# Plain transposes of rows scaled on VectorE, and shifted ticks, in a hybrid encoder trunk

## The chip, the cores and the metric

The kernel runs on one core of a Trainium2 chip. The metric is the device time of one execution in microseconds (us). A core has five engines, each with its own instruction queue that is worked off in order: TensorE (PE in the profile, with PEld for its weight loads), VectorE (DVE), ScalarE (ACT), GpSimd (POOL) and SyncE (SP), which only issues DMAs. Engines wait for one another by semaphores.

## The reference

One layer of a trunk over a sequence of 2048 rows of 1024 numbers, in float32:

```
xn = rmsnorm(x, g1)
u, q, f, i, o, gates = split(xn @ w_in)          # 512 each, gates 2 x 1024
ya = pool_mixer(u) @ w_pa                        # trailing means over 2, 4, 8, 16 rows, minus the row
yb = hgrn2(silu(q), f, i, silu(o)) @ w_pb        # gated linear recurrence, 4 heads of 128
merged = sigmoid(gate_a) * ya + sigmoid(gate_b) * yb
x  = x + merged @ w_o
h  = causal depthwise conv (width 3) of rmsnorm(x, g2) @ w_up    # 2 x 2816 columns
x  = x + (silu(gate half of h) * value half of h) @ w_down
out = rmsnorm(x, final_g)
```

`rmsnorm(x, g) = x * rsqrt(mean(x*x) + eps) * g`, row by row. The recurrence is `S_t = diag(f_t) S_{t-1} + (1 - f_t) i_t^T`, with the output `S_t^T q_t`, normalised and multiplied by silu(o).

## The kernel before

**Tiling.** The sequence is cut into two super-blocks of 1024 rows, and each of these into two halves of 512 rows (four tiles of 128 rows, `NT`). For each super-block `mixer` runs (the input projection, pooling, the recurrence, the two branches, the output projection `wo`), and then `ffn` (the up projection, convolution and gate, the down projection `dn`, and the last norm). The big products go by a scheme of seven products in place of eight on 2x2 blocks, P1 to P7 (`ORDER`, `IO_ORDER`); its operands are forms of the normalised, transposed rows of the two halves: B11 and B21 of the first half, B22 and the sums T1 to T4 of both.

**Precision.** Each operand is split into a high and a low part (the names end in `h` and `l`), and each product is three matmuls, high by high, high by low, low by high, of 128x512. Weights are loaded by SP into `raw`, and converted into `ops` by one instruction on ScalarE (L206, high) and one on VectorE (L207, low). A product of a unit (`Unit.multiply`) is twelve such matmuls: four steps of k by three.

**Order.** Products are written out in order, and their matmuls go through `mm` (L145), which counts them; after every sixth one it calls `tick`. A tick first converts the next weight, at most `LOOKAHEAD` = 4 products ahead, and then steps the tasks: generators, whose `yield n` leaves n ticks before they go on. The tasks issue the forms, the pooling, the recurrence and the last norm between the products' matmuls. The compiler's scheduler then puts each engine's instructions into a final order.

**Norm and transposes.** `norm_rows` takes four tiles of 128 rows (two tiles of 128x512 each): ScalarE squares and sums them (L636, into a tile `junk` that nobody reads), POOL adds the two sums (L637) and makes the reciprocal root (L629, L630), and POOL makes a diagonal matrix of it (L649, `x_dg` or `m_dg`, 128x128). `transpose` then is an ordinary matmul of a 128x128 piece of the rows with the diagonal (L656): it scales and transposes at once, into a PSUM bank (`x_t`, `m_t`). There are eight such blocks of 512 rows: x0 to x3, ahead of the input projection, and m0 to m3, ahead of the up projection, each with 4 x 8 transposes. `forms_a_task` makes the first half's forms, splits included, and `forms_b_task` the second half's (T1 and T2 by L714 from PSUM, then the splits, L607 and L608).  For x0 the transposes are issued row tile by row tile into eight banks (`early`); for the second halves they wait for a signal, `go`, which `ffn` gives ahead of its product number `GO_AT` (`go_up`) and `proj_io` in its second product (`go_io`).

**The gate and value projection.** `proj_io` computes the recurrence's values v and output gates z row-wise, four banks (one for each j) to a product; after P7 it takes `u3 = Z - e1` (L1150, `io_u`), which frees the bank Z for P4's matmuls, and adds it to bank V for z (`out_z`, L999).

**The recurrence.** `hgrn_task` runs eight times in each super-block (four heads, two halves), three at a time. It starts from q and the forget factors f, prepares copies and products on ScalarE and VectorE (L828 to L832), yields, and issues its first products on TensorE (L905, `pl`); its later plain transposes are `pk` (L940) and `pt` (L983), done as `pe.transpose` against the identity.

The functions that the change touches, as they stand:

Of the kernel before, what the change touches and what calls it, by code (L numbers as in the profile page):

```python
# [11 lines left out]
F32 = mybir.dt.float32  # L12
F32R = mybir.dt.float32r
U8 = mybir.dt.uint8
AF = mybir.ActivationFunctionType
ALU = mybir.AluOpType
AX = mybir.AxisListType

P = 128
# [11 lines left out]
NT = TB // P  # L31
# [25 lines left out]

M_ORDER = (0, 4, 1, 5, 2, 6, 3, 7)

N_SLOTS = 80  # L60
N_RUN = 3
N_HEADS = 2
GO_AT = 2
LEAD = 5
X_AT, X_AT2 = 1, 4
GO_IO = (("P2", 1), ("P2", 0))
# [8 lines left out]
MM_PER_TICK = 6  # L75
# [3 lines left out]
def tile_trunk(  # L79
# [16 lines left out]
    pe, act, dve, pool, sp = nc.tensor, nc.scalar, nc.vector, nc.gpsimd, nc.sync  # L96

    const = ctx.enter_context(tc.tile_pool(name="const", bufs=1))
    small = ctx.enter_context(tc.tile_pool(name="small", bufs=8))
    rawp = ctx.enter_context(tc.tile_pool(name="rawp", bufs=N_RAW))  # L100
    opsp = ctx.enter_context(tc.tile_pool(name="opsp", bufs=N_OPS))
    slots = ctx.enter_context(tc.tile_pool(name="slots", bufs=N_SLOTS))
    diags = ctx.enter_context(tc.tile_pool(name="diags", bufs=8))
    dram = ctx.enter_context(tc.tile_pool(name="dram", bufs=1, space=bass.MemoryType.DRAM))
    banks = ctx.enter_context(tc.tile_pool(name="banks", bufs=8, space=bass.MemoryType.PSUM))

    def slot(name, cols=TB, dt=F32):
        return slots.tile([P, cols], dt, tag="s", name=name, padded_shape=[P, 528])

    def bank(name, cols=512):  # L110
        return banks.tile([P, cols], F32, tag="b", name=name, padded_shape=[P, 512])
# [6 lines left out]
    count = [0, None]  # L118
# [15 lines left out]
    def tick():  # L134
        stream.advance(1)
        for t in list(tasks):
            t.wait -= 1
            if t.wait <= 0 and t.live:
                t.step()
# [5 lines left out]
    def mm(*args, **kw):  # L145
        count[1] = pe.matmul(*args, **kw)  # L146
        count[0] += 1
        if count[0] % MM_PER_TICK == 0:
            tick()


# [364 lines left out]
    ident = const.tile([P, P], F32, tag="ident", name="ident")  # L516
# [30 lines left out]
    inv = const.tile([P, 4, 16], F32, tag="inv", name="inv")  # L547
    uhist = const.tile([P, 4, 16], F32, tag="uhist", name="uhist")
    hist = const.tile([P, 2 * MF, 2], F32, tag="hist", name="hist")
    junk = const.tile([P, 512], F32, tag="junk", name="junk")  # L550
    fmask = const.tile([P, 2, 64], F32, tag="fmask", name="fmask")
    state = {}
    state_at = {(0, h) for h in range(HEADS)}
    for h in range(HEADS):
# [65 lines left out]
    def n_step(ps, w, xk, j, first, last, **kw):  # L620
        xh, xl = xk
        a, b = xh[:, j * P : (j + 1) * P], xl[:, j * P : (j + 1) * P]
        mm(ps, a, w[:, 0], start=first, stop=False, **kw)
        mm(ps, a, w[:, 1], start=False, stop=False, **kw)
        mm(ps, b, w[:, 0], start=False, stop=last, **kw)

    def rstd_of(ssq, n, scale, name):
        r = small.tile([P, 4], F32, tag="rstd", name=name)
        pool.tensor_scalar(r[:, :n], ssq, scale, EPS, ALU.mult, ALU.add)  # L629
        pool.tensor_tensor(r[:, :n], r[:, :n], neghalf[:, :n], ALU.pow)  # L630
        return r

    def row_rstd(halves, name):
        ss = small.tile([P, 4], F32, tag="ssq", name=name + "ss")
        for hf in range(2):
            act.activation(junk, halves[hf], AF.Square, accum_out=ss[:, hf : hf + 1])  # L636
        pool.tensor_tensor(ss[:, 2:3], ss[:, 0:1], ss[:, 1:2], ALU.add)  # L637
        return rstd_of(ss[:, 2:3], 1, 1.0 / D, name + "r")

    def norm_rows(src, name, xs, after, lag=1):  # L640
        for j in range(NT):
            while (src, j) not in ready:
                yield 1
            halves = [xt[src, j, c] for c in range(2)]
            r = row_rstd(halves, f"{name}{j}")
            if lag:
                yield lag
            dg = diags.tile([P, P], F32, tag="dg", name=f"{name}dg{j}")
            pool.tensor_scalar(dg, ident, r[:, 0:1], None, ALU.mult)  # L649
            xs[j] = halves, dg  # L650
            after(j)

    def transpose(ps, xs, j, k):
        c = (k % 4) * P
        halves, dg = xs[j]
        pe.matmul(ps[:, j * P : (j + 1) * P], halves[k // 4][:, c : c + P], dg,  # L656
                  start=True, stop=True)

    def transposed(xs, k, name, gain, ps=None):
        if ps is None:  # L660
# [101 lines left out]
    def need(forms, key, late):  # L762
        while len(forms[key]) < 4:
            late.step()
        return forms[key]
# [45 lines left out]
    def hgrn_task(b, h, d, q, vd, zd, od):  # L811
# [18 lines left out]
        dve.tensor_tensor(q1[:, :, 0], qo, do, ALU.mult)  # L830
        dve.tensor_tensor(qe, qe, de, ALU.mult)
        dve.tensor_tensor(qo, q1[:, :, 0], de, ALU.mult)  # L832
        yield 3
        def mask(key, n):
            m = masks[key]
            return m.unsqueeze(1).to_broadcast([P, n, m.shape[1], m.shape[2]])
# [114 lines left out]
        ss = slot(f"ss{b}_{h}")  # L951
# [11 lines left out]
        for c in range(NT):  # L963
            o_ = po[:, c * P : (c + 1) * P]
            pe.matmul(o_, att[:, c * P : (c + 1) * P], vt[:, c * P : (c + 1) * P],
                      start=True, stop=False)
# [3 lines left out]
        for c in range(NT):  # L970
            act.activation(junk[:, c * P : (c + 1) * P], po[:, c * P : (c + 1) * P], AF.Square,
                           accum_out=so[:, c : c + 1])
        r = rstd_of(so, NT, 1.0 / P, f"ro{b}_{h}")
# [10 lines left out]
        t = slot(f"oh{b}_{h}")  # L984
# [6 lines left out]
    def value(dst, a, ps):  # L991
        if a is None:
            act.copy(dst, ps)
            return
        t, how = a
        if how == "from":
            dve.tensor_tensor(dst, ps, t, ALU.subtract)  # L997
        else:
            dve.tensor_tensor(dst, t, ps, ALU.add if how == "add" else ALU.subtract)  # L999

    class Unit:
# [28 lines left out]
        def after(self, p):  # L1030
            bk, t = self.bank, self.t
            if p == "P1":
                act.copy(self.tmp("e1"), bk["X"])  # L1033
            elif p == "P6":
                first(dve.tensor_tensor(self.tmp("u2"), t["e1"], bk["Z"], ALU.subtract))
            elif p == "P2":
                self.emit(0, 0, None, bk["X"])
            elif p == "P7":
                first(dve.tensor_tensor(self.tmp("u3"), bk["Z"], t["e1"], ALU.subtract))
                self.emit(1, 1, (t["u3"], "add"), bk["V"])  # L1040
            elif p == "P4":
                self.emit(1, 0, (t["e1"], "from"), bk["Z"])
            elif p == "P3":
                self.emit(0, 1, (t["u2"], "sub"), bk["V"])
# [76 lines left out]
    def proj_io(b0, forms, late, vd, zd):  # L1121
        bk = {}
        e1, u2, u3 = {}, {}, {}

        def temp(d, key, j):
            d[j] = slot(f"io{b0}_{key}_{j}")
            return d[j]

        def out_v(hf, j, a):
            t = slot(f"v{b0}_{hf}_{j}")  # L1130
            value(t, a, bk["X" if hf == 0 else "V"][j])
            sp.dma_start(vd[hf][:, j, :], t)

        def out_z(hf, j, a):
            t = slot(f"z{b0}_{hf}_{j}")
            g = slot(f"zs{b0}_{hf}_{j}")
            value(t, a, bk["Z" if hf == 0 else "V"][j])
            act.activation(g, t, AF.Sigmoid)
            (dve if hf == 0 else pool).tensor_tensor(t, t, g, ALU.mult)
            sp.dma_start(zd[hf][:, j, :], t)  # L1140

        def after(p, j):
            if p == "P1":
                act.copy(temp(e1, "e1", j), bk["X"][j])
            elif p == "P2":
                out_v(0, j, None)
            elif p == "P6":
                dve.tensor_tensor(temp(u2, "u2", j), e1[j], bk["Z"][j], ALU.subtract)
            elif p == "P7":
                dve.tensor_tensor(temp(u3, "u3", j), bk["Z"][j], e1[j], ALU.subtract)  # L1150
                out_z(1, j, (u3[j], "add"))
            elif p == "P4":
                out_z(0, j, (e1[j], "from"))
            elif p == "P3":
                out_v(1, j, (u2[j], "sub"))

        for p in IO_ORDER:
            xs = need(forms, FORM[p], late)
            kb = BANK[p]
            if kb not in bk:  # L1160
                bk[kb] = [bank(f"io{b0}_{kb}_{j}") for j in range(NT)]
            for k in range(4):
                if (p, k) == GO_IO[b0 > 0]:
                    go_io[0] = True
                w = stream.get("io")
                for j in range(NT):
                    n_step(bk[kb][j], w, xs[k], j, p in FIRST and k == 0, k == 3,
                           skip_group_check=True)
                    if k == 3:
                        after(p, j)  # L1170
                stream.used(1)

    def mixer(b0, forms, late):
# [13 lines left out]
        def runner():  # L1187
            while taken[0] < 2 * HEADS:
                if queue:
                    taken[0] += 1  # L1190
                    yield from hgrn_task(*queue.pop(0))
                else:
                    yield 1
# [186 lines left out]
    def ffn(b0, forms, late):  # L1380
# [113 lines left out]
        for n, (m, p) in enumerate(up_order()):  # L1494
            if n == GO_AT:
                go_up[0] = True
# [119 lines left out]
```

## Time and profile before

| | before |
|---|---|
| median of 3 runs | 2584.07 us (2583.33 to 2585.47) |
| profiled execution | 2583.42 us |
| its span | 2581.7 us, 35951 instructions |
| TensorE busy | 2539.6 us (98%) |
| VectorE busy | 1930.6 us (75%) |
| ScalarE busy | 1196.4 us (46%) |
| POOL busy | 873.9 us (34%) |
| granted TensorE clock, mean | 0.996 |

The span runs from the first to the last instruction in the profile of one execution; the profiled execution's own time is a little longer, and it is this one that a sum over the profile is made against. A row of a group reads: line, engine, operation, output <- inputs with their shapes, count | busy us, mean ns of one | idle time of the engine ahead of them, and what ended it. A row of the timeline: start, duration (us), engine, line, operation, count, and in brackets the idle time ahead with what ended it. Durations of matmuls overlap in the pipeline: their pace is read from start to start.

### The profile page before, as it was taken

The numbers are of one execution on the slowest core, as the hardware profiler recorded it, in microseconds if no ns is written. First come the engines' busy times: TensorE is split into PE (matmuls) and PEld (weight loads), VectorE is DVE, ScalarE is ACT, GpSimd is POOL, SyncE is SP. The second block draws the span as 40 slices with busy tenths as digits, with TensorE's granted clock in tenths as the row PEclk, the third lists the DMA queues.
The fourth block names the chain that finished last, engine by engine and source line by source line (L and its number), as shares of the span: only waits on it lengthen the run. The fifth ranks groups of instructions, "written<-read, shape, count | busy, mean of one in ns | idle before, by whom it ended". The sixth has DMA issues, their size and how long they took to land.

```text
span 2581.7 us, 35951 instructions
## 1 busy us (share of the span) xinstructions
PE 2539.6 (98%) x11720; PEld 2084.1 (81%) x11720; DVE 1930.6 (75%) x3318; ACT 1196.4 (46%) x2244; POOL 873.9 (34%) x1241
## 2 busy tenths in 40 slices
PE   8899999999999999999999999999999999999998
PEld 7678888888788888878888788888887888888887
DVE  6888788587799787785465786775968987778844
ACT  5334434324545554554464354442345554445533
POOL 6544343032454334462241111200233433334512
PEclk9999999999999999999999999999999999999999
DMA  6778768777798889896454343346442454446952
GB/s 230 271 203 226 212 196 250 224 240 225 187 243 236 229 232 238 240 329 232 141 169 141 102 142 112 123 154 228 143 156 91 151 152 146 143 139 207 363 152 98
DMA packets 254060, 496.92 MB, mean 192 GB/s; under 512 B 26736, under 2 KB 43248, under 8 KB 253552
## 3 DMA queue, kind: packets, MB, share of 16 engines
q1 hardware_dynamic: 187968, 319.89, 39.1%
q0 software_dynamic: 41504, 110.64, 16.9%
q10 hardware_dynamic: 24400, 64.08, 7.3%
q8 instruction: 93, 1.52, 0.2%
q14 instruction: 95, 0.78, 0.1%
HBM read 384.94 MB, written 187.17 MB: 222 GB/s over the span
## 4 chain that ended last, share of the span: by engine, by line
PE 53%; DVE 2%; ACT 1%; issue 1%; DMA 1%; POOL 1%; DVEq 0%; POOLq 0%; ACTq 0%; SPq 0%
PE dn_P L146 14%; PE up_Z L146 7%; PE up_V L146 4%; PE up_X L146 4%; PE wo_P L146 3%; PE gr_Z L146 3%; PE gr_V L146 2%; PE gr_X L146 2%; PE pb L146 2%; PE pa L146 2%; PE io_Z L146 1%; PE fr_Z L146 1%; PE fr_X L146 1%; PE fr_V L146 1%; PE io_X L146 1%; PE io_V L146 1%
## 5 line engine op out<-in xcount | busy, mean ns | idle before, releaser
L206 ACT CAST ops<-raw 128x512 fp32r<-128x512 f32 x732 | 452.2, 620 | 757.8 <-PE dn_P L146 126.2
L207 DVE TENSOR_TENSOR ops<-raw,ops 128x512 fp32r<-128x512 f32 x732 | 553.6, 760 | 245.1 <-ACT ops L206 240.4
L1409 DVE SCALAR_TENSOR_TENSOR e<-h,cols,e 128x512 f32<-128x512 f32 x176 | 142.2, 811 | 29.8 <-ACT e L1407 22.2
L1407 ACT ACTIVATE e<-h,cols 128x512 f32<-128x512 f32 x176 | 142.3, 814 | 29.8 <-DVE h L999 21.8
L1412 DVE SCALAR_TENSOR_TENSOR e<-h,cols,e 128x512 f32<-128x512 f32 x176 | 134.7, 774 | 2.8
L1105 POOL TENSOR_TENSOR gf_P<-e,e 128x512 f32<-128x512 f32 x44 | 67.5, 1536 | 153.1 <-DVE e L1418 91.2
L807 POOL DMA_DIRECT2D g_P<-dg_P x154 | 84.4, 549 | 100.8 <-PE dn_P L146 30.5
L1105 POOL TENSOR_TENSOR gf_P<-gf_P,e 128x512 f32<-128x512 f32 x44 | 59.2, 1345 | 66.6 <-DVE e L1418 66.2
L1402 POOL COPY h<-h 128x2 f32<-128x2 f32 x88 | 39.7, 465 | 120.6 <-DVE h L997 118.6
L1404 POOL COPY hist<-h 128x2 f32<-128x2 f32 x88 | 39.2, 446 | 115.9 <-DVE h L999 114.3
L1416 ACT ACTIVATE e<-e 128x512 f32<-128x512 f32 x88 | 55.6, 632 | 49.2 <-DVE e L1412 49.1
L1212 POOL TENSOR_TENSOR q<-q,qs 128x512 f32<-128x512 f32 x16 | 22.5, 1405 | 145.1 <-ACT qs L1211 145.1
L999 DVE TENSOR_TENSOR h<-up_u,up_V 128x512 f32<-128x512 f32 x88 | 60.0, 682 | 12.9 <-PE up_V L146 12.4
L1081 DVE TENSOR_TENSOR x<-x,wo_P 128x512 f32<-128x512 f32 x88 | 55.8, 678 | 17.9 <-PE wo_P L146 17.7
L856 POOL COPY qm<-q 128x64 f32<-128x64 f32 x64 | 24.1, 395 | 131.2 <-DVE q L929 22.1
L1249 ACT ACTIVATE gt<-gt,cols 128x512 f32<-128x512 f32 x48 | 34.8, 724 | 71.3 <-DVE gt L999 59.0
L1081 DVE TENSOR_TENSOR ac<-ac,dn_P 128x512 f32<-128x512 f32 x72 | 47.6, 682 | 18.7 <-PE dn_P L146 16.2
L1105 POOL TENSOR_TENSOR yf_P<-ya,ya 128x512 f32<-128x512 f32 x16 | 21.2, 1331 | 118.7 <-DVE ya L1326 67.7
L1477 POOL TENSOR_TENSOR fss<-fss 128x1 f32<-128x1 f32 x16 | 6.7, 421 | 138.7 <-ACT fo L1467 138.7
L1432 POOL DMA_DIRECT2D dg_P<-gf_P x88 | 50.3, 571 | 8.5 <-POOL gf_P L1105 7.7
L1033 ACT COPY up_e<-up_X 128x512 f32<-128x512 f32 x44 | 25.7, 588 | 55.9 <-PE up_X L146 42.6
L636 ACT ACTIVATE junk<-x 128x512 f32<-128x512 f32 x64 | 40.2, 629 | 23.6 <-DVE x L1081 14.4
(1265 smaller groups left out, 8304.8 us busy)
## 6 DMA issues: line engine op xcount, KB each, us to landing
g_P<-dg_P POOLq DMA_DIRECT2D x154, 256.0 KB, 6.5
raw<-in_w_up_t SPq DMA_DIRECT2D x132, 256.0 KB, 3.3
raw<-in_w_in_t SPq DMA_DIRECT2D x98, 256.0 KB, 3.4
dg_P<-gf_P POOLq DMA_DIRECT2D x88, 256.0 KB, 3.9
raw<-in_w_io SPq DMA_DIRECT2D x68, 256.0 KB, 5.1
dg_P<-e SPq DMA_DIRECT2D x66, 256.0 KB, 3.4
raw<-in_w_dn SPq DMA_DIRECT2D x66, 256.0 KB, 5.3
x<-in_x SPq DMA_DIRECT2D x64, 256.0 KB, 5.2
```

Of the source, the lines that this page charges most:

```text
L146: count[1] = pe.matmul(*args, **kw)
L206: self.mark = act.copy(hi, v)
L207: dve.tensor_tensor(lo, v, f32(hi), ALU.subtract)
L807: eng.dma_start(t, d)
L999: dve.tensor_tensor(dst, t, ps, ALU.add if how == "add" else ALU.subtract)
L1081: dve.tensor_tensor(t, t, ps[j], ALU.add if sg > 0 else ALU.subtract)
L1105: pin(pool.tensor_tensor(t, x0, x1, op))
L1407: in_turn(act.activation(t, h[:, 2:], AF.Identity, bias=col(o_cb + mt), scale=col(o_cw + 4 * MF + mt)))
L1409: in_turn(second(dve.scalar_tensor_tensor(t, h[:, 1 : 1 + TB], col(o_cw + 2 * MF + mt), t, ALU.mult, ALU.add)))
L1412: dve.scalar_tensor_tensor(t, h[:, 0:TB], col(o_cw + mt), t, ALU.mult, ALU.add)
L1416: in_turn(act.activation(g, g, AF.Silu))
L1432: pool.dma_start(d, t)
```

## The change

Rows are scaled ahead of the transposes: `norm_rows` no longer makes a diagonal on POOL. It takes two slots (`x_xs`, `m_xs`), which first take the squares that nobody reads, and VectorE then writes the two scaled half rows into them; `transpose` is now `pe.transpose` of the scaled rows against the identity. The pool of diagonals is gone, and there are two slots more. Ticks fall three matmuls later in the count, in the middle of a product. A recurrence task leaves five ticks instead of three ahead of its first products on TensorE. `GO_AT` goes from 2 to 5: the second half's m transposes are let go three products later. In `proj_io` the four differences of P7 are issued first, each when its bank is complete, and the four sums for z behind the last of them. Two constants change places.

```diff
-N_SLOTS = 80
+N_SLOTS = 82
-GO_AT = 2
+GO_AT = 5
...
-    diags = ctx.enter_context(tc.tile_pool(name="diags", bufs=8))
...
     def mm(*args, **kw):
         count[1] = pe.matmul(*args, **kw)
         count[0] += 1
-        if count[0] % MM_PER_TICK == 0:
+        if count[0] % MM_PER_TICK == 3:
             tick()
...
+    fmask = const.tile([P, 2, 64], F32, tag="fmask", name="fmask")
     junk = const.tile([P, 512], F32, tag="junk", name="junk")
-    fmask = const.tile([P, 2, 64], F32, tag="fmask", name="fmask")
...
-    def row_rstd(halves, name):
+    def row_rstd(halves, junk, name):
         ss = small.tile([P, 4], F32, tag="ssq", name=name + "ss")
         for hf in range(2):
-            act.activation(junk, halves[hf], AF.Square, accum_out=ss[:, hf : hf + 1])
+            act.activation(junk[hf], halves[hf], AF.Square, accum_out=ss[:, hf : hf + 1])
...
             halves = [xt[src, j, c] for c in range(2)]
-            r = row_rstd(halves, f"{name}{j}")
+            t = [slot(f"{name}xs{j}_{hf}") for hf in range(2)]
+            r = row_rstd(halves, t, f"{name}{j}")
             if lag:
                 yield lag
-            dg = diags.tile([P, P], F32, tag="dg", name=f"{name}dg{j}")
-            pool.tensor_scalar(dg, ident, r[:, 0:1], None, ALU.mult)
-            xs[j] = halves, dg
+            for hf in range(2):
+                dve.tensor_scalar(t[hf], halves[hf], r[:, 0:1], None, ALU.mult)
+                xs[j, hf] = t[hf]
             after(j)
 
     def transpose(ps, xs, j, k):
         c = (k % 4) * P
-        halves, dg = xs[j]
-        pe.matmul(ps[:, j * P : (j + 1) * P], halves[k // 4][:, c : c + P], dg,
-                  start=True, stop=True)
+        pe.transpose(ps[:, j * P : (j + 1) * P], xs[j, k // 4][:, c : c + P], ident)
...
         dve.tensor_tensor(qo, q1[:, :, 0], de, ALU.mult)
-        yield 3
+        yield 5
...
                 dve.tensor_tensor(temp(u3, "u3", j), bk["Z"][j], e1[j], ALU.subtract)
-                out_z(1, j, (u3[j], "add"))
+                if j == NT - 1:
+                    for i in range(NT):
+                        out_z(1, i, (u3[i], "add"))
```

How the change moves instructions is seen in the final order of each engine. In it a row has the line, the operation, the output and the inputs with the programs' numbers, and the shape; the changed kernel's lines are one or two lower.

TensorE at the first products of the recurrence in the first super-block; `gr_0_Z` is the bank of product P6 of a gate unit and `gr_0_V` that of P5, `pl` the recurrence's products for the two halves. Before:

```order
L146 MATMUL gr_0_Z<-x_T23h,ops_1423 128x512
L146 MATMUL gr_0_Z<-x_T23l,ops_1423 128x512
L146 MATMUL gr_0_Z<-x_T23h,ops_1423 128x512
L905 MATMUL pl_0_1_1545<-q_0_1499,k_0_1495 128x128 x4
L905 MATMUL pl_0_1_1555<-q_0_1512,k_0_1508 128x128 x4
L146 MATMUL gr_0_V<-x_T10h,ops_1442 128x512
```

and in the changed kernel:

```order
L145 MATMUL gr_0_Z<-x_T23h,ops_1433 128x512
L145 MATMUL gr_0_V<-x_T10h,ops_1452 128x512
L145 MATMUL gr_0_V<-x_T11h,ops_1452 128x512
L145 MATMUL gr_0_V<-x_T11l,ops_1452 128x512
L145 MATMUL gr_0_V<-x_T11h,ops_1452 128x512
L145 MATMUL gr_0_V<-x_T12h,ops_1452 128x512
L145 MATMUL gr_0_V<-x_T12l,ops_1452 128x512
L145 MATMUL gr_0_V<-x_T12h,ops_1452 128x512
L145 MATMUL gr_0_V<-x_T13h,ops_1452 128x512
L145 MATMUL gr_0_V<-x_T13l,ops_1452 128x512
L145 MATMUL gr_0_V<-x_T13h,ops_1452 128x512
L903 MATMUL pl_0_1_1578<-q_0_1509,k_0_1505 128x128 x4
```

The two `pl` groups stood between P6 and P5; now they stand behind P5, ten of whose matmuls follow P6's last one (its other two stand within P6).

VectorE behind product P7 of `proj_io` in the first super-block; `io_u` are the differences, `z` the sums. Before:

```order
L608 TENSOR_TENSOR x_B223l<-x_b_627,x_B223h 128x512
L1150 TENSOR_TENSOR io_u_0_1037<-io_Z_694,io_e_0_431 128x512
L999 TENSOR_TENSOR z_1_0_1039<-io_u_0_1037,io_V_830 128x512
L1150 TENSOR_TENSOR io_u_1_1053<-io_Z_695,io_e_1_441 128x512
L999 TENSOR_TENSOR z_1_1_1055<-io_u_1_1053,io_V_831 128x512
L1150 TENSOR_TENSOR io_u_2_1064<-io_Z_696,io_e_2_446 128x512
```

and in the changed kernel:

```order
L607 TENSOR_TENSOR x_B223l<-x_b_637,x_B223h 128x512
L1148 TENSOR_TENSOR io_u_0_1055<-io_Z_707,io_e_0_449 128x512
L1148 TENSOR_TENSOR io_u_1_1060<-io_Z_708,io_e_1_454 128x512
L1148 TENSOR_TENSOR io_u_2_1065<-io_Z_709,io_e_2_465 128x512
L1148 TENSOR_TENSOR io_u_3_1070<-io_Z_710,io_e_3_470 128x512
L997 TENSOR_TENSOR z_1_0_1072<-io_u_0_1055,io_V_843 128x512
```

The first difference keeps its place behind the split of the form B22; the other three move ahead of the sums.

TensorE at the start of the FFN of the first super-block, where the second half's transposes begin; `up_1_X` is a product P1 of unit 1. Before:

```order
L146 MATMUL up_1_X<-m_f3l,ops_6380 128x512
L146 MATMUL up_1_X<-m_f3h,ops_6380 128x512
L656 MATMUL m_t_6592<-m_dg_6426,x_0_0_5508 128x128
L656 MATMUL m_t_6592<-m_dg_6474,x_1_0_5551 128x128
L656 MATMUL m_t_6597<-m_dg_6426,x_0_1_5510 128x128
```

and in the changed kernel:

```order
L145 MATMUL up_3_X<-m_f0l,ops_6594 128x512
L145 MATMUL up_3_X<-m_f0h,ops_6594 128x512
L655 MATMUL m_t_6678<-ident,m_xs_0_6454 128x128
L655 MATMUL m_t_6678<-ident,m_xs_0_6487 128x128
L655 MATMUL m_t_6678<-ident,m_xs_0_6530 128x128
```

They began behind the second product of the FFN (P1 of unit 1), and begin now three matmuls into the sixth (P1 of unit 3), with scaled rows and the identity in place of rows and diagonals.

## The prediction

> **What bounds the kernel now.** First the page: busy time by engine, and the chain of work that ended last.
>
> ```profile
> span 2581.7 us, 35951 instructions
> ...
> PE 2539.6 (98%) x11720; PEld 2084.1 (81%) x11720; DVE 1930.6 (75%) x3318; ACT 1196.4 (46%) x2244; POOL 873.9 (34%) x1241
> ...
> PE 53%; DVE 2%; ACT 1%; issue 1%; DMA 1%; POOL 1%; DVEq 0%; POOLq 0%; ACTq 0%; SPq 0%
> ```
>
> TensorE works 98% of the span. So time taken off its stream shortens the kernel almost one for one, and another engine matters only where TensorE waits for it. Next the waits of TensorE (total us, times, longest):
>
> ```profile
> PE x_t L656 <- POOL x_dg L649: 9.8, 3, 7.5
> PE io_Z L146 <- DVE io_u L1150: 5.1, 1, 5.1
> PE pl L905 <- ACT q L828: 4.1, 3, 2.2
> PE pl L905 <- DVE q L830: 3.2, 1, 3.2
> ...
> PE pl L905 <- ACT gr_e L1033: 1.5, 1, 1.5
> ```
>
> They name the places of the change: the row transposes, the gate differences, and the recurrence's first products (4.1 + 3.2 + 1.5 = 8.8 us). Then the transposes by group, and as they stand in the stream:
>
> ```profile
> L656 PE MATMUL x_t<-x_dg,x 128*128 128x128 f32 x256 | 34.7, 291 | 9.8 <-POOL x_dg L649 9.8
> L656 PE MATMUL m_t<-m_dg,x 128*128 128x128 f32 x256 | 32.7, 275 | 0.0
> ```
> ```profile
> 29.89 3.73 PE L656 MATMUL x_t<-x_dg,x 128*128 128x128 f32 x32
> ...
> 282.99 0.60 PE L940 MATMUL pk<-ident,k 128*128 128x128 f32 x4
> 283.35 0.48 PE L146 MATMUL fr_X<-x_f6h,ops 128*128 128x512 f32 x1
> 283.66 0.39 PE L146 MATMUL fr_X<-x_f6l,ops 128*128 128x512 f32 x1
> ```
>
> Eight blocks of rows (x and m, four each) with 32 transposes apiece are 256 transposes, and there are 512 records: an ordinary f32 matmul against the diagonal is two passes. The key row is the fourth: `pk` in the recurrence is already a plain transpose against the identity, four of them for a head, and has four records: one pass.
>
> **The transposes.** 32 records end 3.73 us after the first begins; less one duration (0.275), 3.45/31 = 0.111 us a record, so 0.223 us for a transpose now. The plain one: (0.60 - 0.275)/3 = 0.108. The matmul behind the `pk` group starts the next one 0.31 us later, an ordinary one every 0.23 (below, 2.79 us for 12), so no cost of a switch beyond 0.1 us a group shows; I neglect it. The saving is 0.223 - 0.108 = 0.114 us each, 29.2 us for 256, and nothing if the new form still takes two passes (a rival). For the blocks m0 to m3, x2 and x3 (192 transposes) I book 192 x 0.114 = **21.9 us** in full: they stand among products of a TensorE that is hardly waiting there (0.0 of idle time in the m row). x0 and x1 come next, by themselves. The Trainium skill, "TensorE: Matmul & The Clock Gate", section "Part 4: PE-mode transpose", gives about 275 ns for a transpose in a kernel's context; taken as the pace, the sum would be an estimated 256 x 0.052 = 13 us longer than now instead of 29 shorter. The `pk` row speaks against taking it so: 275 ns is about the duration of one, and four in a row are done in 600.
>
> **What VectorE takes over.** 32 rows get two scalings of 128x512 each, 64 instructions; POOL loses 32 diagonals. No scaling of this form stands in the trace. Neighbours:
>
> ```profile
> L830 DVE TENSOR_TENSOR q<-q,f 128x256 f32<-128x256 f32 x16 | 7.8, 485 | 0.0
> ...
> L1081 DVE TENSOR_TENSOR x<-x,wo_P 128x512 f32<-128x512 f32 x88 | 55.8, 678 | 17.9 <-PE wo_P L146 17.7
> L207 DVE TENSOR_TENSOR ops<-raw,ops 128x512 fp32r<-128x512 f32 x732 | 553.6, 760 | 245.1 <-ACT ops L206 240.4
> ```
>
> A scaling reads 512 numbers a partition, as the first row does (two operands of 256): 0.49 us; at most 0.68, the full-width row. 64 x 0.49 = 31 us (44 at most) on VectorE: 1931 + 31 = 1962 of some 2557, 77%. TensorE's matmuls cover it everywhere but where VectorE is the last to end. These places follow.
>
> **Start, x0 and x1.** Stretches of the start (columns: length, then busy time of PE, PEld, DVE, ACT, POOL, granted clock, DMA share, GB/s), and its end:
>
> ```profile
> 8.00:17.60 9.60, 9.60 (x65) 9.49 (x64) 3.83 (x7) 7.28 (x18) 6.41 (x11) 1.00 1.05 394
> 17.60:49.50 31.90, 30.51 (x162) 25.11 (x161) 22.12 (x32) 16.89 (x36) 28.86 (x56) 1.00 0.52 177
> 49.50:82.60 33.10, 33.10 (x143) 26.93 (x144) 29.18 (x38) 20.96 (x37) 15.47 (x11) 1.00 0.77 273
> 82.60:92.00 9.40, 4.34 (x12) 3.12 (x11) 9.26 (x16) 1.95 (x4) 2.44 (x2) 0.64 0.31 105
> ```
> ```profile
> 87.28 0.67 DVE L1150 TENSOR_TENSOR io_u<-io_Z,io_e 128x512 f32<-128x512 f32 x1
> ...
> 88.59 0.69 DVE L1150 TENSOR_TENSOR io_u<-io_Z,io_e 128x512 f32<-128x512 f32 x1
> ```
> ```profile
> 88.10 1.19 PE L146 MATMUL io_Z<-ops,x_T40h 128*128 128x512 f32 x2 [5.06 <-DVE io_u L1150]
> ...
> 91.96 0.40 PE L146 MATMUL io_Z<-ops,x_T43h 128*128 128x512 f32 x1
> ```
>
> x0's 32 transposes stand in the first stretch, where rows still arrive; x1's in the second. 64 x 0.114 = 7.3 us come off TensorE. But VectorE is busy 29.2 of 33.1 us in the third stretch and 9.3 of 9.4 in the fourth, where TensorE waits 5.06 us for the first difference, which stands behind VectorE's backlog of forms. Behind that wait nine matmuls take 3.86 us instead of 2.1, at a granted clock of 0.64: 1.8 us more. If TensorE runs ahead and VectorE doesn't, the gain ends in that wait; x1's eight scalings, 8 x 0.49 = 3.9 us, even stand in VectorE's busy time. Differences first changes little at this point: the first difference is first in both orders, and the second, ready at 89.28, comes before TensorE is through the first bank's products. Bounds: -9 (7.3, and the 1.8) to +4 (all swallowed, and x1's scalings on top). Between them I take **-3**, some half of the gross gain, as VectorE isn't the bound until some 50 us.
>
> **Recurrence chains.** The first products of the two heads that stall:
>
> ```profile
> 144.66 1.13 PE L905 MATMUL pl<-q,k 128*128 128x128 f32 x8 [3.19 <-DVE q L830]
> 146.57 2.08 PE L905 MATMUL pl<-q,k 128*128 128x128 f32 x8 [0.77 <-ACT q L828]
> ...
> 1421.82 1.16 PE L905 MATMUL pl<-q,k 128*128 128x128 f32 x8 [1.08 <-ACT q L828]
> ...
> 1425.21 1.16 PE L905 MATMUL pl<-q,k 128*128 128x128 f32 x8 [2.23 <-ACT q L828]
> ```
>
> Two ticks more are 12 matmuls; in the order of the changed kernel ten of P5 now stand ahead of `pl`, 10 x 0.231 = 2.3 us of cover for each pair. Pairs wait 3.96, 3.31 and (the table) 1.5 us: 2.3 + 2.3 + 1.5 = 6.1. Bounds: nothing (the chain is late by something else) to -12 (8.8, and two slow spells of 1.8 like the one above, rounded down). I take **-6**. That each head ends two ticks later costs nothing: the next head's work and the products stand in between.
>
> **Starts of the FFN.** The second half's m transposes go three products later.
>
> ```profile
> 652.53 1.28 PE L656 MATMUL m_t<-m_dg,x 128*128 128x128 f32 x10
> ...
> 677.08 0.40 PE L146 MATMUL up_Z<-m_T20h,ops 128*128 128x512 f32 x1
> ...
> 679.41 0.39 PE L146 MATMUL up_Z<-m_T23l,ops 128*128 128x512 f32 x1
> ...
> 679.87 0.40 PE L146 MATMUL up_Z<-m_T20h,ops 128*128 128x512 f32 x1
> ```
> ```profile
> 655.46 0.75 DVE L714 SCALAR_TENSOR_TENSOR m_t<-m_t,cols,m_b 128x512 f32<-128x512 f32 x1 [0.90 <-PE m_t L656]
> ...
> 669.36 1.24 DVE L608 TENSOR_TENSOR m_T23l<-m_t,m_T23h 128x512 fp32r<-128x512 f32 x1 [0.69 <-ACT m_T23h L607]
> ```
>
> The last two rows of the first fence give a product: 2.79 us. T23l is done at 670.60, needed at 679.41: 8.8 us of slack. Three products are 8.4 us, and the shorter transposes (32 x 0.114 = 3.6) bring TensorE to the need earlier: 8.8 - 8.4 - 3.6 = -3.2, a wait. The forms come sooner too, since `m_t`'s banks fill in half the time (1.8 us sooner for the first pair): some 1.5 us of wait, twice, **+3**. Bounds: nothing (their ticks follow TensorE) to 9 (two of 3.2, and what queues behind on VectorE).
>
> **x2 and x3**, in front of the second super-block:
>
> ```profile
> 1286.16 0.20 POOL L637 TENSOR_TENSOR x_0ss<-x_0ss 128x1 f32<-128x1 f32 x1 [4.91 <-ACT junk L636]
> ...
> 1287.37 0.61 POOL L649 TENSOR_SCALAR x_dg<-ident,x_0r 128x128 f32<-128x128 f32 x1
> ```
> ```profile
> 1293.45 0.49 PE L656 MATMUL x_t<-x_dg,x 128*128 128x128 f32 x2 [1.33 <-POOL x_dg L649]
> ...
> 1296.00 1.16 PE L656 MATMUL x_t<-x_dg,x 128*128 128x128 f32 x8 [0.91 <-POOL x_dg L649]
> ```
>
> TensorE waits 2.2 us for diagonals. Two scalings (0.98) in place of one diagonal (0.61), and up to one conversion (0.76) ahead of them on VectorE, make a row 1.1 us later: **+1**; bounds -2 (the waits vanish) to +4 (1.1 at each of four rows).
>
> Ticks in the middle of a product add no instruction. They move the issue of tasks and conversions by three matmuls, 0.7 us, against a lead of four products, 11 us: 0, its sign unknown, inside the bounds above. Moved squares and constants: 0.
>
> **Sum.** 2583.42 (the profiled execution; its span is 2581.7) - 21.9 - 3 - 6 + 3 + 1 = 2556.5; the median of the runs shown, 2584.07, is 0.65 above: **2557 us**. All ends together: 2539 to 2579.
>
> **The rivals.**
> A is the forecast, with 2550 to 2564 of its own: 0.55.
> B, VectorE and the forms take their share: x0 and x1 give nothing, the FFN starts cost 9, x2 and x3 4: 2583.4 - 21.9 + 9 + 4 - 6 + 0.65 = 2569. For it the 9.3 of 9.4 us at the end of the start; against it VectorE at 75% otherwise: 0.17.
> C, the stalls go wholly: x0 and x1 pay 9, the chains 12: 2583.4 - 21.9 - 9 - 12 + 3 + 1 + 0.65 = 2545. For it the clock of 0.64 behind a stall; against it the VectorE backlog: 0.14.
> D, plain transposes don't hold the granted clock up, and each of the eight blocks is followed by a slow spell of some 1.6 us: 13 us, 2570. Against it the two matmuls behind `pk`, 0.31 us and then the usual pace: 0.04. The same section of the Trainium skill says that transposes aren't counted as a busy TensorE by its clock gate; by that rule the spells come, and the trace doesn't agree with it for groups of four.
> E, slower: a scaling waits at the head of VectorE's queue for POOL's chain of the row (1286.16 to 1287.37, 1.2 us), and the conversions behind it, L207, wait too. If each of 32 rows blocks VectorE so and TensorE has no lead, 32 x 1.2 = 38 us come on: 2595. It decides from the point where the blocks of a group outrun the lead of 11 us. Four rows are under 5 us: 0.05.
> F, the change doesn't do what it says: transposes still have two records. 29.2 us fall away, the chains remain: 2583.4 - 6 + 3 + 1 + 0.65 = 2582. Against it `pk`: 0.05.
>
> **How the numbers follow.** Differences under 0.2% (5 us) can't be told from none. A to D are faster: 0.90; F is the same: 0.05; E slower: 0.05. The range holds A, most of B and of C: 2545 to 2572.
>
> **What would show it.** Right: 256 records of the row transposes in place of 512, at 0.11 us each; some 64 scalings of 0.4 to 0.7 us; `pl` waits of under 3 us in all; VectorE at 77%. Wrong: waits of TensorE on `up_Z` above 9 us in all; waits for L207 that weren't there; the `io_Z` wait above 9 us; a granted clock under 1 behind transposes.

## The result: 0.44% faster, less than half of the forecast

| | before | after |
|---|---|---|
| median | 2584.99 us (8 runs, 2582.71 to 2586.57) | 2572.93 us (8 runs, 2570.28 to 2579.11) |
| ratio | | 0.9956, 95% interval 0.9945 to 0.9967 |
| profiled execution | 2583.42 us | 2575.64 us |
| its span | 2581.7 us | 2573.9 us |

The gain is 12 us; 27 were forecast, and the time lies 0.9 us above the range. The profiled execution after is 2.7 us above its median, so the traces differ by 7.8 us only.

The page of the changed kernel:

```profile
span 2573.9 us, 35491 instructions
...
PE 2519.3 (98%) x11464; PEld 2057.0 (80%) x11464; DVE 1964.0 (76%) x3382; ACT 1191.9 (46%) x2244; POOL 851.5 (33%) x1209
```

256 TensorE instructions are gone and 64 of VectorE are new; VectorE's 1964 us are the 1962 foretold. The transposes and the scalings by group, and then four transposes as they stand in the stream:

```profile
L655 PE MATMUL x_t<-ident,x_xs 128*128 128x128 f32 x128 | 20.1, 303 | 8.8 <-DVE x_xs L649 8.8
L655 PE MATMUL m_t<-ident,m_xs 128*128 128x128 f32 x128 | 18.2, 272 | 0.0
...
L649 DVE TENSOR_SCALAR x_xs<-x,x_3r 128x512 f32<-128x512 f32 x8 | 5.3, 698 | 0.9 <-POOL x_3r L629 0.9
...
L649 DVE TENSOR_SCALAR m_xs<-x,m_0r 128x512 f32<-128x512 f32 x8 | 3.5, 482 | 5.2 <-POOL m_0r L629 5.2
```
```profile
640.03 0.60 PE L655 MATMUL m_t<-ident,m_xs 128*128 128x128 f32 x4
```

One record for a transpose, (0.60 - 0.272)/3 = 0.109 us: the saving of 29 us on TensorE's stream is real. Scalings took 0.48 to 0.70 us by the means of their groups. So the missing time must be in waits, and in what follows them. The waits of TensorE after (total us, times, longest):

```profile
PE x_t L655 <- DVE x_xs L649: 8.8, 2, 7.8
PE fr_Z L145 <- DVE ops L206: 4.5, 1, 4.5
PE io_Z L145 <- DVE io_u L1148: 4.3, 1, 4.3
PE io_X L145 <- ACT io_e L1142: 3.5, 2, 3.0
PE gr_Z L145 <- DVE gr_u L1033: 3.3, 2, 2.4
PE up_Z L145 <- ACT m_T23h L606: 2.6, 2, 1.3
PE io_X L145 <- POOL x_f0h L604: 2.4, 1, 2.4
PE up_Z L145 <- DVE m_T23l L607: 2.3, 2, 1.1
...
PE pl L903 <- ACT q L826: 1.9, 2, 1.2
...
PE pl L903 <- DVE q L828: 1.5, 1, 1.5
...
PE up_V L145 <- DVE m_T12l L607: 1.1, 2, 0.8
```

The recurrence's first products wait 3.4 us where they waited 8.8. But seven of these rows are new or longer: splits, conversions, differences and copies of VectorE and ScalarE, and x0's first form on POOL, for which TensorE hadn't waited, or not so long. Summed over all starts of matmuls that come more than 0.15 us later than the pace of their form (0.231 us for 512 columns, 0.111 for 128), TensorE loses 36.9 us before and 58.9 after: 22 of the 29 us went there, and the rest is about the 7.8 us by which the spans differ. Some 8 of the 22 aren't waits but matmuls that start at half rate behind a wait; the mean granted clock fell from 0.996 to 0.993.

By stage, in us between the first matmuls of one stage and the next, read from the traces (e5, e6, e9 and e15 are experiments below; "1" and "2" are the super-blocks):

| stage | before | after | e5 transposes only | e6 scalings only | e9 three pairs | e15 best |
|---|---|---|---|---|---|---|
| start and `proj_io`, 1 | 110.6 | 113.7 | 112.3 | 115.4 | 114.6 | 108.7 |
| gates, recurrence, 1 | 352.9 | 356.7 | 353.0 | 353.5 | 350.9 | 352.9 |
| `wo`, 1 | 85.2 | 81.3 | 81.5 | 84.8 | 81.3 | 81.5 |
| up, 1 | 432.7 | 434.5 | 434.1 | 433.5 | 428.8 | 428.9 |
| down, 1 | 230.9 | 227.3 | 228.6 | 234.2 | 227.4 | 226.9 |
| `proj_io`, 2 | 85.0 | 82.6 | 81.5 | 85.1 | 82.7 | 84.2 |
| gates, recurrence, 2 | 342.9 | 338.5 | 343.2 | 343.2 | 339.2 | 339.2 |
| `wo`, 2 | 85.3 | 81.2 | 81.6 | 85.0 | 81.2 | 81.3 |
| up, 2 | 431.9 | 433.5 | 433.8 | 433.9 | 429.8 | 428.6 |

How far one profile can be trusted: the changed kernel and the three experiments e2, e9 and e10 have the same code up to the branches of the first super-block, and reach them at 470.4, 469.3, 465.5 and 465.2 us; e13, which has the code of the kernel before up to the FFN, takes 359.9 us in the second row, not 352.9. So differences of up to 7 us in that row are not a finding. The rows of the second super-block repeat within 1 us among kernels with the same code there, those of `up` within 2 us: the changed kernel, e8 and e12 have 434.5, 435.5 and 434.3 us in the first and 433.5, 433.2 and 432.1 in the second.

### The profile page after: what moved, and what is told of

Its sections match the earlier page's. It is cut to its first block, busy times and chain, and to the rows that moved or that the text cites. A ratio compares the mean times of both kernels' runs of the same rounds, so it can differ in the third digit from the quotient of the medians.

```text
span 2573.9 us, 35491 instructions
## 1 busy us (share of the span) xinstructions
PE 2519.3 (98%) x11464; PEld 2057.0 (80%) x11464; DVE 1964.0 (76%) x3382; ACT 1191.9 (46%) x2244; POOL 851.5 (33%) x1209
## 3 DMA queue, kind: packets, MB, share of 16 engines
q0 software_dynamic: 41504, 110.64, 16.8%
## 4 chain that ended last, share of the span: by engine, by line
PE 89%; DVE 5%; issue 2%; ACT 2%; DMA 1%; POOL 1%; SPq 0%; DVEq 0%; POOLq 0%; ACTq 0%
PE dn_P L145 16%; PE up_Z L145 14%; PE up_V L145 9%; PE up_X L145 9%; PE wo_P L145 6%; PE gr_Z L145 5%; PE pb L145 3%; PE pa L145 3%; PE gr_X L145 3%; PE gr_V L145 3%; PE fr_Z L145 3%; PE fr_V L145 2%; PE fr_X L145 2%; PE pl L867 1%; PE io_Z L145 1%
```

## Experiments

All were timed in five rounds beside the kernel before, whose median was 2584.0 to 2584.9 us in these jobs. The first four part the rows from the moves.

**e1, the row part alone** (changed kernel, with the other four parts undone):

```diff
-GO_AT = 5
+GO_AT = 2
-        if count[0] % MM_PER_TICK == 3:
+        if count[0] % MM_PER_TICK == 0:
-        yield 5
+        yield 3
-                if j == NT - 1:
-                    for i in range(NT):
-                        out_z(1, i, (u3[i], "add"))
+                out_z(1, j, (u3[j], "add"))
```

> The kernel before with the row part alone: rows scaled on VectorE, plain transposes, 82 slots; ticks, recurrence yield, GO_AT and the order in proj_io as before. Theory M (the moves of work, above all the later start of the second half's m transposes, open the new stalls; the transposes pay in full): the 29 us come off and only the start loses some, 2557 to 2563 us. Rival V (the scalings on VectorE open the new stalls by themselves): 2568 to 2575 us, with waits of TensorE on up_Z and fr_Z as in the changed kernel.

Measured: 2587.86 us, ratio 1.0008 (0.9999 to 1.0018). By itself the row part gains nothing that can be told from noise. Both theories had it faster; the rival is nearer, and it too is off by 13 us.

**e2, `GO_AT` back at 2.**

```diff
-GO_AT = 5
+GO_AT = 2
```

> The changed kernel with GO_AT back at 2. Theory M: TensorE's lost time at the two starts of the FFN falls from about 8 and 7 us (waits on m_T23 and m_T1, and the half clock behind them) to about 3 each, so 9 us less: 2564 us. Rival V: the waits on m_T23 and m_T1 stay, 2571 to 2575 us.

Measured: 2573.83 us, ratio 0.9957 (0.9944 to 0.9969): as the changed kernel. Theory M falls in this point. The wait on T23 is gone, but TensorE waits about as long one step earlier, in the timeline of e2 at the first start of the FFN:

```profile
674.60 0.54 PE L145 MATMUL up_X<-m_f4h,ops 128*128 128x512 f32 x1 [4.78 <-ACT up_e L1031]
```

`up_e` is the copy that empties the bank X of a unit for its P2. It stands behind the high part of T23 in ScalarE's queue, which waits for VectorE's T2.

**e3, ticks on the sixth matmul.**

```diff
-        if count[0] % MM_PER_TICK == 3:
+        if count[0] % MM_PER_TICK == 0:
```

> The changed kernel with ticks on the sixth matmul again. Theory M with the tick as one of the moves: the waits for conversions (fr_Z on L206, 4.6 us and 2.3 of half clock; the wait inside x0's forms) fall back to those of before, 2564 to 2568 us. Rival V: the tick is nothing, 2571 to 2575 us, and fr_Z still waits more than 4 us.

Measured: 2576.48 us, ratio 0.9971 (0.9961 to 0.9981): some 3 us slower than the changed kernel by the medians (the intervals overlap by a little), not faster. Neither expectation holds in full: `fr_Z` waits 2.8 us instead of 4.5, so the shifted tick does cost at that place, but it gives as much or more elsewhere.

**e4, all moves without the rows** (kernel before, with the opposite edits of e1).

> The kernel before with all other parts of the change and without the row part: diagonals on POOL and two-pass transposes stay, the tick is shifted, the recurrence yields 5, GO_AT is 5, the differences come first. Theory M: it carries the new stalls without the gain, 2588 to 2598 us. Rival V: it has the recurrence's gain alone, 2574 to 2580 us.

Measured: 2592.08 us, ratio 1.0029 (1.0018 to 1.0040), as theory M had it. So the row part alone is worth +2 to +3 us (not clear of nothing), the moves alone +7, and both together -12: the parts are not additive, and no sum of parts gives the result. The next two take the row part itself to pieces.

**e5, one-pass transposes alone.** The rows go unscaled, so this kernel leaves out the norm's factor; a 0/1 diagonal is made on POOL from the same root:

```diff
-            pool.tensor_scalar(dg, ident, r[:, 0:1], None, ALU.mult)
+            pool.tensor_scalar(dg, ident, r[:, 0:1], 0.0, ALU.mult, ALU.is_gt)
...
-        pe.matmul(ps[:, j * P : (j + 1) * P], halves[k // 4][:, c : c + P], dg,
-                  start=True, stop=True)
+        pe.transpose(ps[:, j * P : (j + 1) * P], halves[k // 4][:, c : c + P], dg)
```

> The kernel before with one-pass transposes and nothing else: POOL makes a 0/1 diagonal from the same reciprocal root with the same instruction count (so TensorE waits as before), the rows go unscaled, and VectorE gets no scaling. What is left out is the norm's factor in the rows. Theory L (TensorE only arrives sooner at forms and bank releases that come from VectorE's and ScalarE's queues at their own time): of 29 us a third to a half stays, 2570 to 2576 us, with longer waits on up_e and io_e. Rival V (the scalings cost what the transposes save): 2555 to 2561 us.

Measured: 2576.28 us, ratio 0.9969 (0.9959 to 0.9979): 8 us of 29, a little less than theory L says. TensorE's waits in e5:

```profile
PE up_X L146 <- ACT up_e L1032: 8.0, 2, 4.2
...
PE io_Z L146 <- DVE x_t L713: 3.2, 1, 3.2
```

Without a single scaling, 8.0 us are lost on `up_e` (0.9 before) and 3.2 on T2 at the start (1.1 before). The two waits on `up_e` were 0.46 and 0.42 us and are 4.19 and 3.82: they grew by 3.7 and 3.4 us, which is the 3.6 that 32 shorter transposes save. TensorE came to that point sooner by the whole saving, and waited it away. Where the transposes are shortened in `wo`, `down` and `proj_io` 2 the stages are 2.3 to 3.7 us shorter (32 x 0.114 = 3.6); at the start and in both `up` stages they aren't.

**e6, the scalings alone**, written to slots that nobody reads, diagonals and two-pass transposes as before:

```diff
             xs[j] = halves, dg
+            for hf in range(2):
+                dve.tensor_scalar(slot(f"{name}xs{j}_{hf}"), halves[hf], r[:, 0:1], None, ALU.mult)
```

> The kernel before with the 64 scalings on VectorE added, written to slots that nobody reads; diagonals and two-pass transposes stay. Theory L: VectorE has room, 2585 to 2591 us. Rival V: it is slower by 15 us and more, 2600 us, with the new waits at the start and at the starts of the FFN.

Measured: 2593.84 us, ratio 1.0033 (1.0020 to 1.0046): +9, between the two. In the table 4.8 of it are at the start, 3.3 where x2's rows come, and 2.0 in the second `up`. So 8 us of gain (e5) and 9 of cost (e6) fit with the rows alone (e1) being worth nothing. e6 also takes 64 more slots out of the 80; what of the 9 us that costs, it doesn't show.

**e7, the recurrence's yield back at 3.**

```diff
-        yield 5
+        yield 3
```

> The changed kernel with the recurrence's first yield back at 3. If the longer yield brings what the chain of waits promised (5 to 6 us): 2577 to 2581 us, with pl waits of 8 to 10 us in all. If it only moves waits to later products (the gr_Z waits on gr_u, 3.3 us, would go): 2571 to 2575 us.

Measured: 2600.14 us, ratio 1.0056 (1.0041 to 1.0072). Both expectations miss: 27 us slower than the changed kernel. Waits of TensorE in e7, and then the group of VectorE's differences that empty the bank Z of a gate unit behind P7, first in e7, then in the changed kernel:

```profile
PE gr_Z L145 <- DVE gr_u L1037: 6.9, 5, 2.9
PE pl L903 <- DVE q L828: 6.0, 3, 3.2
```
```profile
L1037 DVE TENSOR_TENSOR gr_u<-gr_Z,gr_e 128x512 f32<-128x512 f32 x16 | 11.2, 700 | 0.7 <-PE gr_Z L145 0.7
```
```profile
L1037 DVE TENSOR_TENSOR gr_u<-gr_Z,gr_e 128x512 f32<-128x512 f32 x16 | 11.0, 689 | 21.1 <-PE gr_Z L145 21.1
```

The idle time ahead of the group is the reading: in the changed kernel VectorE stands ready and waits 21 us for TensorE's products; in e7 it comes to them out of other work (0.7), and TensorE waits for it. The short yield does this only together with the shifted tick: the same group has 14.2 us of idle time ahead of it in the kernel before, 14.5 in e1 and 19.1 in e3. Of the 27 us, 8.5 are in the second super-block's gates and recurrence, and 10.7 in the first's, where one profile says less. With e1 and e3 this makes a square (all with the new rows; e1 also has `GO_AT` 2 and the old order of sums, worth nothing by e2 and e12):

| | yield 3 | yield 5 |
|---|---|---|
| tick on the sixth | 2587.9 (e1) | 2576.5 (e3) |
| tick on the third | 2600.1 (e7) | 2572.9 (changed) |

The tick costs 12 us with the short yield and gains about 3 with the long one; the yield gains 11 or 27. They act as one edit: where the recurrence's bursts fall against the ends of products.

**e8, x1's norm issued earlier.** The start's new wait on `io_e` is a matter of ScalarE's order. ScalarE and then TensorE in the changed kernel:

```profile
24.93 0.62 ACT L205 CAST ops<-raw 128x512 fp32r<-128x512 f32 x1 [6.69 <-PE io_X L145]
...
27.13 0.63 ACT L635 ACTIVATE x_xs<-x 128x512 f32<-128x512 f32 x1
...
32.03 2.01 ACT L1142 COPY io_e<-io_X 128x512 f32<-128x512 f32 x4
```
```profile
32.74 0.71 PE L145 MATMUL io_X<-ops,x_f4h 128*128 128x512 f32 x2 [3.00 <-ACT io_e L1142]
```

ScalarE idles 6.7 us ahead of a conversion that waits for an operand buffer, then makes x1's eight squares (27.1 to 32.0), and only then the copies that TensorE needs. Before, the squares stood between x0's evacuations, ahead of that conversion.

```diff
     load_rows(1)
+    for _ in range(5):
+        nxt[1].step()
+    nxt[2].step()
     join(nxt[1])
```

> The changed kernel with x1's norm (squares on ScalarE, scalings) issued behind x0's fifth form, in ScalarE's idle time, and not behind all eight. Theory A (ScalarE's order at the start: the squares stand ahead of the copies io_e that free the bank): the wait of 3.0 us and the slow spell of 1.4 behind it go, 2567 to 2570 us. Rival (VectorE's backlog up to the io_Z wait takes it back): 2572 to 2575 us, with a longer io_Z wait.

Measured: 2571.58 us, ratio 0.9947 (0.9933 to 0.9962). The `io_e` wait is gone and the start takes 109.8 us instead of 113.7 in the profiles; in the median it is 1.4 us, which can't be told from nothing.

**e9, three pairs of units ahead of the first P6.**

```diff
-N_HEADS = 2
+N_HEADS = 3
```

> The changed kernel with three pairs of units, not two, whose products P1 and P2 stand ahead of the first P6 in the FFN: the need for T2 comes four products (11 us) later. Theory L (at a start of the FFN the forms of VectorE are the last to come; shorter transposes only bring TensorE to that wait sooner): the lost 6.3 and 5.0 us at up_Z and up_V (m_T23, m_T11, m_T12) go, 2561 to 2566 us. Rival: the forms are late by the tick and stay as late against the products, or two more open units hold slots and banks: 2571 to 2577 us.

Measured: 2564.67 us, ratio 0.9925 (0.9911 to 0.9938): 8.3 us less than the changed kernel, as theory L had it. The waits on T23, T11 and T12 are gone; at that start of the FFN the timeline of e9 has this left:

```profile
677.19 0.50 PE L145 MATMUL up_X<-m_f4h,ops 128*128 128x512 f32 x1 [0.33 <-ACT up_e L1031]
```

**e10, `GO_AT` at 4.**

```diff
-GO_AT = 5
+GO_AT = 4
```

> The changed kernel with GO_AT at 4: the forms start 2.8 us sooner. If the start of the forms sets the wait: the T2 waits fall by 2.8 us at each start less what up_e takes, 2568 to 2571 us. If the forms' own work sets it (as 2 for GO_AT gave the same time as 5): 2572 to 2575 us, the wait only going from m_T23 to up_e.

Measured: 2575.92 us, ratio 0.9968 (0.9956 to 0.9981); nothing gained. With 2 and 4 the wait is on `up_e`, with 5 on T23: it only changes its name.

**e11, scalings on ScalarE.**

```diff
-                dve.tensor_scalar(t[hf], halves[hf], r[:, 0:1], None, ALU.mult)
+                act.activation(t[hf], halves[hf], AF.Copy, scale=r[:, 0:1])
```

> The changed kernel with the 64 scalings on ScalarE (0.6 us each) in place of VectorE. Added alone to the kernel before, VectorE's scalings cost 9 us. If VectorE's queue is what they cost: 2564 to 2568 us. If any engine in the forms' chain is as bad (ScalarE makes squares, evacuations, high parts and conversions there): 2571 to 2580 us.

Measured: 2590.11 us, ratio 1.0020 (1.0011 to 1.0029): worse than either expectation, 17 us slower than on VectorE. Being at 46% over the span says nothing of a chain in which ScalarE makes squares, evacuations and high parts one behind the other: the first transposes wait 10.1 us instead of 7.8.

**e12, sums and differences interleaved.**

```diff
-                if j == NT - 1:
-                    for i in range(NT):
-                        out_z(1, i, (u3[i], "add"))
+                out_z(1, j, (u3[j], "add"))
```

> The changed kernel with the sums for z interleaved with the differences again. As predicted (the first difference is first in both orders): no change, 2571 to 2575 us. If the order frees the banks for P4 sooner: 2576 to 2580 us, with waits of io_Z behind the first one.

Measured: 2571.00 us, ratio 0.9951 (0.9938 to 0.9963): no difference, as predicted.

**e13, three pairs in the kernel before**: the edit of e9 alone.

> The kernel before with three pairs of units ahead of the first P6, and nothing else. Theory L: before, TensorE waited only 0.6 us at each start of the FFN, so there is next to nothing to win: 2582 to 2586 us. Rival (the longer head is faster by itself): 2574 to 2578 us.

Measured: 2584.10 us, ratio 1.0000 (0.9992 to 1.0009). So the 8 us of e9 are time that the changed kernel's transposes had opened and that the forms had held back; before there was nothing to win. By stage, e9's two `up` are 3.9 and 2.1 us shorter than before, where the changed kernel's are 1.8 and 1.6 longer.

**e14 and e15, joined**: e9 with e8, and with e12 too.

> The changed kernel with three pairs of units and x1's squares issued earlier: 8.3 and 1.4 us less than the changed kernel if the two are independent, 2562 to 2564 us; 2565 to 2568 if the second is nothing.

> The same, with the sums for z interleaved with the differences again as in the kernel before: 1 to 2 us less than with the differences first, 2560 to 2563 us; the same or more if that order was nothing.

Measured: 2559.17 us, ratio 0.9903 (0.9890 to 0.9916), and 2555.86 us, ratio 0.9885 (0.9871 to 0.9899). e15 beats both kernels, by 17 us the changed one. Both lie below what was expected. The two can't be told apart by their intervals. e14 is some 4 us below the sum of its parts, so e8 may be worth more than its own run shows.

**e16, old rows for x0 and x1 alone** (diagonals, two-pass transposes, no scalings there).

```diff
+            if old:
+                dg = diags.tile([P, P], F32, tag="dg", name=f"{name}dg{j}")
+                pool.tensor_scalar(dg, ident, r[:, 0:1], None, ALU.mult)
+                xs[j] = halves, dg
+                after(j)
+                continue
```

> The changed kernel with diagonals and two-pass transposes for x0 and x1 alone (64 transposes, 16 scalings and 8 diagonals go back). If the forms at the start swallow the gain and the scalings cost some: 2568 to 2573 us, with fr_X reached near 110.6 us as before. Rival (the transposes pay there too): 2577 to 2581 us.

Measured: 2577.53 us, ratio 0.9965 (0.9953 to 0.9978). The two parts of the first expectation part company: the start takes 112.6 us, no longer than the changed kernel's 113.7 though 64 transposes are slow again; but the whole is slower, at the time of the rival, with some 7 us lost at 401 to 412 us in the recurrence (a transpose `pt` waits 4.5 us), which the changed kernel doesn't have. e4 has the same wait, 4.8 us at 401 us; like e16 it has diagonals for x0 and x1 beside the shifted tick and the longer yield. The runs of e16 spread from 2565.59 to 2581.46 us. That the start swallows the gain agrees with e5 and e6; what an edit at the start does to the recurrence 300 us later is not explained by these runs.

## Why the prediction was wrong

Between forecast (-26.9) and profile (-7.8) 19 us are missing: 7.6 in the two `up` stages, 6.1 at the start, and the rest in the first super-block's gates and recurrence, where one profile says little. The nearest account on record is rival B, whose time, 2569, still was 4 us short: it has the waits at the starts of the FFN and nothing gained at the start nearly right, and a cost at x2 and x3 that didn't come.

**The saving per transpose: right.** 0.114 us foretold, 0.223 - 0.109 measured. Rival F falls. The Trainium skill, "TensorE: Matmul & The Clock Gate", section "Part 4: PE-mode transpose", gives about 275 ns for a transpose in a kernel's context. One here lasts 272 ns, but in the stream one follows another every 109 ns. Rival D has no slow spell behind the transposes among products in its favour. At the start it isn't settled: behind x0's transposes and a wait of 2.4 us the granted clock was 0.50 from 16.8 to 20.2 us, where it was 1.00 before. e5 has this too behind a wait of 0.7 us, and e1 doesn't behind one of 2.8, so no run tells the transposes from the wait.

**192 x 0.114 "in full": the step that failed.** For m0, m2, x2 and x3 it holds: the two `wo` stages are 3.9 and 4.1 us shorter, `down` 1 and `proj_io` 2 together 6.0. For m1 and m3 it doesn't. Their transposes stand among products, and TensorE wasn't waiting there, but it was hardly ahead of the forms: the prediction's own rows give 8.8 us of slack at T23. With 32 transposes shorter by 3.6 us and a start 8.4 us later this is overdrawn, which the text computed (-3.2) and then softened to 1.5 a start. And the slack was not one: undoing the late start (e2) changes nothing, since the forms' chain on VectorE also holds `up_e` in ScalarE's queue. There TensorE already waited in the kernel before, a little at each start of the FFN, by a row that the prediction doesn't use:

```profile
PE up_X L146 <- ACT up_e L1033: 0.9, 2, 0.5
```

With no slack at that point, 3.6 us saved ahead of it are 3.6 us more of waiting, as e5 shows, and the half rate behind the wait comes on top. Measured, the `up` stages are 1.8 and 1.6 us longer where 2.1 shorter was forecast: 7.6 us missing. e9 and e13 settle this cause. The sign named for it, waits on `up_Z` above 9 us in all, didn't come: they are 7.9 us, and the half rate behind a wait doesn't count as waiting. In the changed kernel a wait of two pieces at T23 is followed by half-rate matmuls, which were not in the sum:

```profile
679.97 0.51 PE L145 MATMUL up_Z<-m_T23h,ops 128*128 128x512 f32 x1 [1.29 <-ACT m_T23h L606]
681.61 0.51 PE L145 MATMUL up_Z<-m_T23l,ops 128*128 128x512 f32 x1 [1.14 <-DVE m_T23l L607]
...
682.84 0.63 PE L145 MATMUL up_Z<-m_T20h,ops 128*128 128x512 f32 x1
...
685.40 0.59 PE L145 MATMUL up_Z<-m_T22h,ops 128*128 128x512 f32 x1
```

Here a matmul starts every 0.43 us; seven of them lose 1.4 us.

**Start: -3 foretold, +3.1 measured.** The bounds, -9 to +4, held it; the value taken was on the wrong side. In e2, e9 and e10, whose code is the same up to there, the start has +6.1, +4.0 and +3.6, so it isn't known more closely than that. The prediction read VectorE's backlog and the `io_Z` wait rightly (4.3 us remain) but reasoned that VectorE isn't the bound until 50 us. It overlooked ScalarE, whose order the change turned over (e8), and x0's first form: TensorE now waits 2.4 us for `x_f0h` on POOL, and goes on at the half clock. In the experiments the transposes alone give +1.7 there and the scalings alone +4.8.

**Chains: -6 foretold, 2.3 of it in the second super-block; measured -4.4 there, and nothing certain in the first** (353 us before, 350.9 to 356.7 in the five profiles of the changed kernel and of e2, e9, e10 and e12, which have the same recurrence). The waits on `pl` fell by 5.4 us, near the 6.1 worked out from the cover, to 3.4 and not under 3. In the second super-block a spell at half rate behind `pl` (granted clock 0.50 from 1426.4 to 1429.8 us before, 1.00 after) went with them. But one sentence beside it failed. "Ticks in the middle of a product ... 0": the tick is worth +12 or -3 by the yield. With the shifted tick the longer yield does more than give ten matmuls of cover: it keeps VectorE's bursts out of the way of the differences (e7); with the old tick they weren't in the way. That the tick, booked at 0, does no harm in the changed kernel hangs on this pairing, which the prediction didn't see.

**Scalings, "TensorE's matmuls cover it everywhere but where VectorE is the last to end": too cheap.** Their durations were right, their price was not: 9 us by themselves (e6), where the sum had charged them only through the ends of terms. Rival E, a queue blocked at each row, is too strong; but its direction is what e6 shows. In the changed kernel VectorE stands idle ahead of the scalings for 19.3 us, in 20 waits for POOL's reciprocal root, where E had 38.

**`GO_AT` as the cause of the FFN's +3, and io differences:** worth nothing either way (e2, e10, e12).

Still open: what the change does to the first super-block's gates and recurrence, why e4 and e16 lose time there, and how the start's loss divides among the scalings, ScalarE's order and the half clock.

## What to carry to other kernels

A saving on the busiest engine counts only as far as its next inputs are early: for every stretch that gets shorter, find the instruction that it feeds or waits for next, and its slack, and stop counting there. Then move the need (three pairs, e9) rather than the start of the supply: that turned a 12 us gain into 19, and 26 to 29 with the start put in order as well (e14, e15). And where tasks are stepped by a counter, its phase and the yields are one setting that can weigh more than the instructions saved; test them as a square, not one by one.

## What the runs showed of the hardware

Past the start, every wait of TensorE of 2.9 us and more, 30 of them in the eighteen traces, was followed by matmuls at half rate, under a granted clock of 0.50. Between 1.9 and 2.8 us it went either way (2.1 us on `fr_Z` before: none; 2.4 on `gr_Z` after: seven matmuls; 2.8 on `fr_Z`: none in e1, a spell in e3). Two waits of 1.3 and 1.1 us ahead of two successive matmuls did it too at both starts of the FFN after, but not at the second one in e8. Where matmuls of 512 columns followed, a spell cost 1.3 to 2.7 us, so that a wait of 3 us is one of 4 to 6. In the changed kernel the wait at `fr_Z` shows it:

```profile
124.48 0.80 PE L145 MATMUL fr_Z<-x_T20h,ops 128*128 128x512 f32 x1 [4.45 <-DVE ops L206]
125.07 0.63 PE L145 MATMUL fr_Z<-x_T21h,ops 128*128 128x512 f32 x1
...
128.91 0.63 PE L145 MATMUL fr_X<-x_f4h,ops 128*128 128x512 f32 x1
```

Starts are 0.43 us apart for ten matmuls in place of 0.23; the granted clock is 0.50 from 122.6 to 129.4 us.
